# Weight splits that run further ahead into space that MoBA's values, outputs and softmax weights take later, in a two-layer trunk (mLSTM, MoBA)

## The chip, the cores and the metric

One core of a Trainium2 chip. The metric is the device time of one execution of the whole kernel in microseconds, as the median of several runs. The profile is of one further execution.

## What is computed

A residual trunk of two layers on 256 tokens of width 1024, all inputs float32. Each layer adds a token mixer and then a SwiGLU FFN of inner width 2816. Layer 0's mixer is a chunkwise mLSTM with 4 heads, layer 1's is MoBA block attention with 8 heads of 128; with 256 tokens there is one block, so it is causal attention with normed and partly rotated queries and keys.

```python
for layer in range(DEPTH):                       # DEPTH = 2
    u = rmsnorm(h, norm_mix[layer])
    y = mlstm_mixer(u, ...) if layer == 0 else moba_mixer(u, positions, ...)
    h = h + y
    h = h + swiglu(rmsnorm(h, norm_ffn[layer]), ffn_w_in[layer], ffn_w_out[layer])

def moba_mixer(u, positions, w_in, g_q, g_k, w_out):
    q, k, v = jnp.split(u @ w_in, 3, axis=-1)
    qh = rotary(rmsnorm(split_heads(q, h), g_q), positions, ROPE_DIMS, ROPE_THETA)
    kh = rotary(rmsnorm(split_heads(k, h), g_k), positions, ROPE_DIMS, ROPE_THETA)
    ...
    return merge_heads(softmax(causal(qh @ kh.T * scale)) @ vh) @ w_out
```

## The kernel before

**Products in three parts.** Every float32 product is made of float16 parts: a value is split into a high part h and a rest l, and the product is h·h + h·l + l·h, three matmuls into one PSUM bank. Matmuls are 128x128 against 512 columns; the activations are the stationary side (PEld), the weights move.

**Weight pieces.** All weight matrices are cut into 98 pieces of 1 MB (128 partitions x 2048 float32), in the order of use, the list `specs`. Layer 0 uses pieces 0 to 48, layer 1 pieces 49 to 97. Within a layer there are 12 pieces of the mixer's input projection, 4 of its output projection, 22 of the FFN's input and 11 of its output. In MoBA pieces 49 to 52 are queries and keys of the first four heads, 53 to 56 those of the others, 57 to 60 the values, 61 to 64 the output projection; 65 is the first of the second FFN.

**The class `Weights`** (from line 261) takes each piece through three stages. `load` and `quarter` bring it from HBM in four DMAs of 256 KB (a quarter), issued on SP's queue, into one of 5 buffers `raw`. `high` (line 286) makes half of the high part on ACT (`wh`, 128x1024), `low` (line 295) half of the rest on DVE (`wl`, 128x1024). So a piece costs two instructions on each of the two engines; pieces 0 and 1, at the start, are made in chunks by the hand-written list `START`. The split parts lie in a ring of `WBUFS` = 8 pieces (tags `wh` and `wl`). `take` hands pieces to a stage that is about to use them, and makes at once what isn't split yet; `free` gives them back once their last matmul is written. An output projection takes four pieces and frees them together at its end; the FFN's output stage frees its first seven one at a time and its last four, the tail, together.

**The order of the work** is set when the program is built, by a planner. `Pace` keeps a modelled time, `spend` advances it by the time of each group of matmuls, and after each such step it runs jobs that have come due. Chains (class `Chain`) are short sequences of DVE and ACT steps, such as a norm or a softmax; each step is due when its input is ready by the model. After each step `Weights.ahead` (line 312) may put in up to two quarters of loads, one `low` and one `high`. A split is put in only if its engine is free in the model and no chain step of that engine is due within `near` us (`pace.due`). `near` and `room` depend on the lead, the number of pieces split and not yet taken (line 321). Norm chains carry a margin of 1.25 us of their own, which `due` uses if it is larger than `near`. At the end, `in_queue_order` ties each engine's instructions to the order in which they were written. The instructions of SP's queue are in that order too: weight quarters, and the transposing DMAs.

**Flips.** `flip16` (line 510) transposes 16-bit tiles by DMA, on SP's queue. It follows the last step of a norm chain (`norm`, line 448), writing the next stage's activations `u` (`u_f<-n` in front of the FFNs, `u_b<-n` in front of MoBA), of MoBA's query and key chains (`bqT`, `bkT`), of softmax (`pT`) and of the FFN's hidden values (`h<-n`). The tile names of the profile are by the first program line that used a buffer, so that the norm's tile in front of layer 1's FFN is shown as `u_b<-x,r,grow`, and that in front of MoBA as `u_f<-x,r,grow`.

**The stages around the change.** `ffn(0, ...)`: the hidden stage (`gu`), then the output stage (`f0o`), then two norm chains, one for each token tile of 128. MoBA: `b` (query and key projections) with the chains of `qk_norm` (line 1054), the scores `s` and softmax chains of `softmax` (line 1113), `bv` (values, `v_done`, line 1108), `o` (attention times values, `attend_b`, line 1167), and `bo` (the output projection, `out_proj`, line 857). `out_proj` does token tile 0 first, adds the residual (`residual_half`), and starts its norm chain while PE works on token tile 1; then `ffn(1, ...)` begins with token tile 0 of the first hidden block. MoBA's tiles stand in the pool `pb`, among them the values `vb` (high and rest), the outputs `oh` and `ol`, and `pT` with 6 buffers.

```python
            lead = self.lows // 2 - self.taken
            near, room = (-9.0, 0.35) if lead < 2 else (0.7, 0.35) if lead < 3 else (1.6, 0.2) if lead < 5 else (3.0, 0.0)
            if self.lows < self.highs and pace.free["DVE"] <= pace.now + room and self.split[self.lows] < pace.now + 0.3 \
                    and not pace.due("DVE", near):
                self.low()
            if self.highs < 2 * (self.freed + WBUFS) and pace.free["ACT"] <= pace.now + room \
                    and self.loaded(self.highs // 2) and not pace.due("ACT", near):
                self.high()
```

Of the kernel before, what the change touches and what calls it, by code (L numbers as in the profile page):

```python
# [12 lines left out]
F16 = mybir.dt.float16  # L13
# [7 lines left out]
P = 128  # L21
D = 1024
KD = D // P
S = 256
NT = S // P
# [33 lines left out]
RAWBUFS, WBUFS = 5, 8  # L59
# [134 lines left out]
def in_queue_order(tc):  # L194

    last = {}
    for i in list(tc.nc.cur_bb.bb.instructions):
        if i.engine in last:
            tc.add_manual_dep(i, last[i.engine].name,
                              mybir.DependencyInfo(mybir.DependencyClass.NoSync, mybir.DependencyReason.DATA),  # L200
                              reason="queue order")
        last[i.engine] = i
# [3 lines left out]
def trunk(ctx: ExitStack, tc: tile.TileContext, a: dict, out: bass.AP):  # L206
    pace = Pace()
# [3 lines left out]
    wpool = ctx.enter_context(tc.tile_pool(name="wpool", bufs=1))  # L211
# [8 lines left out]
    def ybank(name):  # L220
        return py.tile([P, 512], F32, tag="y", name=name)

    def mm(dst, lhsT, rhs, start, stop):
        nc.tensor.matmul(dst, lhsT, rhs, start=start, stop=stop)  # L224
# [27 lines left out]
    specs = []  # L252
# [8 lines left out]
    class Weights:  # L261
        def __init__(self):
            self.raws, self.parts = [], []
            self.highs = self.lows = self.taken = self.freed = 0
            self.owed, self.landed, self.split = 0, {}, {}
            self.quarters = []

# [18 lines left out]
        def high(self):  # L286

            i, sl = self.highs // 2, self.half(self.highs)
            if i == len(self.parts):
                self.parts.append([wpool.tile([P, 2048], F16, tag=f"w{x}", bufs=WBUFS, name=f"w{x}{i}") for x in "hl"])  # L290
            nc.scalar.activation(self.parts[i][0][:, sl], self.raws[i][:, sl], AF.Copy, scale=WS)
            self.split[self.highs] = pace.end
            self.highs += 1
# [9 lines left out]
        def load_owed(self, whole=False):  # L303
            if self.owed and len(self.raws) < len(specs):
                self.load(whole)
                self.owed -= 1

        def loaded(self, i):

            return i < len(self.raws) and not any(q[0] <= i for q in self.quarters) and self.landed.get(i, 0.0) < pace.now + 0.3  # L310

        def ahead(self):

            for _ in range(2):
                if not self.quarters:
                    self.load_owed()
                if self.quarters and pace.free["DMA"] < pace.now + 0.5:
                    self.quarter()

            lead = self.lows // 2 - self.taken  # L320
            near, room = (-9.0, 0.35) if lead < 2 else (0.7, 0.35) if lead < 3 else (1.6, 0.2) if lead < 5 else (3.0, 0.0)
            if self.lows < self.highs and pace.free["DVE"] <= pace.now + room and self.split[self.lows] < pace.now + 0.3 \
                    and not pace.due("DVE", near):
                self.low()
            if self.highs < 2 * (self.freed + WBUFS) and pace.free["ACT"] <= pace.now + room \
                    and self.loaded(self.highs // 2) and not pace.due("ACT", near):
                self.high()

# [21 lines left out]
    ws = Weights()  # L350
# [45 lines left out]
    def new_u(name):  # L396

        both = act.tile([P, KD, 2, S], F16, tag="u16", bufs=1, name=f"u16_{name}")
        return both[:, :, 0, :], both[:, :, 1, :], both
# [110 lines left out]
    def flip16(dst, src):  # L510

        nc.sync.dma_start(dst, src, transpose=True)
        pace.work("DMA", 1.9, 1.3)
# [37 lines left out]
    for half in range(2):  # L551
        h = wpool.tile([P, 2048], F16, tag="wh", bufs=WBUFS, name=f"wh{half}")
# [3 lines left out]
    w = ws.take_k(2, 4)  # L556
# [173 lines left out]
    for g in range(2):  # L730
        w = ws.take_k(2, 4)
# [80 lines left out]
    for i in range(2):  # L812
        if i == 1:
            w = ws.take_k(2, 4)
# [34 lines left out]
    for i in range(2):  # L849
        w = ws.take_k(2, 4)  # L850
# [6 lines left out]
    def out_proj(name, y, ready, u_next, grow):  # L857

        w = []
        banks = [[xbank(f"{name}o{t}{n}") for n in range(2)] for t in range(NT)]  # L860

        def part(t, ks, ns=(0, 1)):
            for k in ks:
                if len(w) <= k:
                    w.extend(ws.take_k(1, 2))
                ready(t, k)
                acc_chunk(banks[t], *y(k), w[k], t, k == 0, k == KD - 1, ns)


        half = KD // 2  # L870
        part(0, range(half))
        part(1, range(half), (0,))
        ss = new_ss(0)
        sums = []
        for n in range(2):
            part(0, range(half, KD), (n,))
            sums.append(residual_half(0, n, banks[0][n], 1.0 / PS, ss))
        j0 = norm(name, 0, ss, grow, u_next, sums)
        ss = new_ss(1)
        sums = []  # L880
        for n in range(2):
            part(1, range(half if n == 0 else 0, KD), (n,))
            sums.append(residual_half(1, n, banks[1][n], 1.0 / PS, ss))
        j0()
        ws.free(4)
        return norm(name, 1, ss, grow, u_next, sums)
# [153 lines left out]
    def middle():  # L1040
        pace.later(1.0, rope_tables)

    u_next = new_u("b")
    j1 = ffn(0, u, j1, u_next, a["norm_mix"][1], middle)
    u = u_next
# [2 lines left out]
    pool_b = tc.tile_pool(name="pb", bufs=1)  # L1048
    pb = pool_b.__enter__()
    qkT = [pb.tile([P, 2, 8, S], F16, name=f"b{n}T") for n in "qk"]  # L1050
    vb = [pb.tile([P, NT, D], F16, name=f"vb{x}") for x in "hl"]
    tjobs = {}

    def qk_norm(g, i, t, b):
# [58 lines left out]
    def softmax(h):  # L1113

        for t in range(NT):
            for g in range(2):
                tjobs[g, h // 4, t].finish()
        b = ybank(f"s{h}")
        (qh, ql), (kh, kl) = [(x[:, h // 4, h % 4], x[:, h // 4, 4 + h % 4]) for x in qkT]
        for t in range(NT):  # L1120
            dst = b[:, t * P:t * P + (t + 1) * P]
            sl, ks = slice(t * P, (t + 1) * P), slice(0, (t + 1) * P)
            mm(dst, qh[:, sl], kh[:, ks], True, False)
            mm(dst, qh[:, sl], kl[:, ks], False, False)
            mm(dst, ql[:, sl], kh[:, ks], False, False)
            mm(b[:, 2 * t * P:(2 * t + 1) * P], identb, neg_ts, False, True)
        pace.spend(0.6)
        mx = small.tile([P, NT], F32, name="mx")
        p = pb.tile([P, 384], F32, tag="p", bufs=4, name="p")
        sm = small.tile([P, NT], F32, name="sm")  # L1130
        rs = small.tile([P, NT], F32, name="rsm")
        p16 = pb.tile([P, 2, 384], F16, tag="p16", bufs=3, name="p16")
        cols = (slice(0, 128), slice(128, 384))

        def biggest():
            for t in range(NT):
                nc.vector.tensor_reduce(mx[:, t:t + 1], b[:, cols[t]], axis=AX.X, op=ALU.max, negate=True)

        def exps():
            for t in range(NT):  # L1140
                nc.scalar.activation(p[:, cols[t]], b[:, cols[t]], AF.Exp, bias=mx[:, t:t + 1], accum_out=sm[:, t:t + 1])

        def factor():
            nc.vector.tensor_scalar(sm, sm, 1.0 / PSC, None, op0=ALU.mult)
            nc.vector.reciprocal(rs, sm)

        def high():
            for t in range(NT):
                nc.scalar.activation(p16[:, 0, cols[t]], p[:, cols[t]], AF.Copy, scale=rs[:, t:t + 1])

        def low():
            for t in range(NT):
                nc.vector.scalar_tensor_tensor(p16[:, 1, cols[t]], p[:, cols[t]], rs[:, t:t + 1], p16[:, 0, cols[t]],
                                               op0=ALU.mult, op1=ALU.subtract)
            pT = pb.tile([P, 2, 3, P], F16, tag="pT", bufs=6, name=f"pT{h}")
            flip16(pT.rearrange("p x c s -> p (x c) s"), p16.rearrange("p x n -> p (x n)"))
            pts[h] = [pT[:, x].rearrange("p c s -> p (c s)") for x in range(2)]

        last[0] = pace.now
        pace.end = pace.now + 0.15  # L1160
        fjobs[h] = Chain(pace, [("DVE", biggest), ("ACT", exps), ("DVE", factor), ("ACT", high), ("DVE", low)], True)

    fjobs = {}
    oh = pb.tile([P, KD, S], F16, name="oh")
    ol = pb.tile([P, KD, S], F16, name="ol")

    def attend_b(hp):
        b = ybank(f"o{hp}")
# [41 lines left out]
    for i in range(2):  # L1210
        w = ws.take_k(2, 4)
# [13 lines left out]
    u = new_u("f1")  # L1225
    j1 = out_proj("b", lambda k: (oh[:, k, :], ol[:, k, :]), ready_b, u, grow)
    pool_b.__exit__(None, None, None)
    ffn(1, u, j1, None, None, None)
    in_queue_order(tc)

# [20 lines left out]
```

## Time and profile before

| what | us |
|---|---|
| median of 3 runs | 551.24 |
| the runs | 548.90, 551.24, 552.22 |
| the profiled execution's own time | 550.87 |
| its span, from the first to the last instruction | 548.7 |
| PE busy in the span | 537.6 |
| DVE busy | 355.4 |
| ACT busy | 313.2 |

The profile's times are counted from the start of the span. PE is TensorE's matmuls, PEld its weight loads, DVE VectorE, ACT ScalarE, SPq the queue of the engine that issues the DMAs. A matmul's end is modelled and matmuls overlap, so 512 columns are shown as 0.38 us while one starts every 0.216 us. The waits name what ended an idle time: of several awaited things the one that came last by the profile. The chain of waits is followed back from the last instruction. "To landing" is the time from a DMA's issue to the arrival of its data. Nearly all instructions stand at one of two helper lines (L180 for ACT, DVE and POOL, L224 for matmuls), so the tile names tell them apart.

### The profile page before, as it was taken

How to read it: one execution, taken by the hardware profiler on the slowest of the kernel's cores; microseconds unless marked ns; L12 is line 12 of the kernel's file. 1: busy time of each engine (PE TensorE's matmuls, PEld its weight loads, DVE VectorE, ACT ScalarE, POOL GpSimd, SP SyncE). 2: the span in 40 equal slices, each digit the busy share in tenths (PEclk: the TensorE clock that was granted, in tenths of full speed). 3: DMA queues.
4: the chain of work that ended last, by engine and by line, in shares of the span. 5: the costliest groups of instructions: out<-in, count | busy, mean ns of one | idle time of the engine just before them, and what ended most of it. 6: DMA issues, size and time to landing. Idle time of an engine off the chain costs nothing.

```text
span 548.7 us, 7762 instructions
## 1 busy us (share of the span) xinstructions
PE 537.6 (98%) x2650; PEld 251.3 (46%) x2650; DVE 355.4 (65%) x540; ACT 313.2 (57%) x548; POOL 49.9 (9%) x105
## 2 busy tenths in 40 slices
PE   6999999999999999999999999998999999999997
PEld 2454654344444444444444455543444444444443
DVE  3889799478767665673358788998656647656201
ACT  5876794375466555563268996866455556456100
POOL 3600070020300000000013320000000000000000
PEclk8999999999999999999999999999999999999999
DMA  8999969959699787799328969798698888889002
GB/s 299 352 271 257 361 162 266 307 108 225 168 266 265 208 238 227 233 383 378 122 53 229 258 153 271 134 325 173 187 246 228 225 226 231 224 236 339 9 0 76
DMA packets 140679, 122.33 MB, mean 223 GB/s; under 512 B 66472, under 2 KB 111536, under 8 KB 140640
## 3 DMA queue, kind: packets, MB, share of 16 engines
q1 hardware_dynamic: 139904, 119.58, 77.6%
q0 software_dynamic: 736, 2.27, 1.5%
q8 instruction: 20, 0.33, 0.2%
q14 instruction: 19, 0.16, 0.1%
HBM read 106.08 MB, written 1.05 MB: 195 GB/s over the span
## 4 chain that ended last, share of the span: by engine, by line
PE 96%; DMA 1%; issue 1%; POOL 1%; DVE 0%; ACT 0%; SPq 0%; POOLq 0%; ACTq 0%
PE gu L224 42%; PE f1o L224 10%; PE f0o L224 10%; PE b L224 8%; PE ao L224 7%; PE av L224 4%; PE bo L224 4%; PE bv L224 4%; PE ak L224 2%; PE aq L224 2%; PE s L224 1%; PE num L224 1%; PE o L224 1%; DMA u_f<-n 1%; DMA x<-in_x 1%
## 5 line engine op out<-in xcount | busy, mean ns | idle before, releaser
L180 DVE SCALAR_TENSOR_TENSOR wl<-raw,wh 128x1024 f16<-128x1024 f32 (+1 forms) x200 | 236.9, 1203 | 43.0 <-ACT wh L180 41.5
L180 ACT ACTIVATE wh<-raw 128x1024 f16<-128x1024 f32 (+1 forms) x200 | 202.5, 1041 | 75.2 <-DMA raw<-in_ffn_w_in 32.9
L224 PE MATMUL gu<-wh,u_f 128*128 128x512 f16 x704 | 209.8, 379 | 3.1 <-DVE wl L180 1.9
L224 PEld LDWEIGHTS <-u_f 128*128 128x128 f16 x1056 | 103.2, 98 | 128.2 <-DMA u_f<-n 4.1
L224 PE MATMUL gu<-wl,u_f 128*128 128x512 f16 x352 | 133.4, 379 | 0.0
L224 PEld LDWEIGHTS <-h 128*128 128x128 f16 x528 | 51.7, 98 | 62.3
L180 DVE SCALAR_TENSOR_TENSOR fh<-gu,fsg 128x256 f32<-128x256 f32 x44 | 18.7, 425 | 55.9 <-ACT fsg L180 55.9
L224 PE MATMUL f1o<-wh,h 128*128 128x512 f16 x176 | 46.6, 379 | 0.0
L224 PE MATMUL f0o<-wh,h 128*128 128x512 f16 x176 | 46.6, 379 | 0.0
L224 PEld LDWEIGHTS <-u_a 128*128 128x128 f16 x336 | 29.2, 99 | 35.9 <-ACT u_a L180 3.1
L224 PEld LDWEIGHTS <-u_b 128*128 128x128 f16 x288 | 27.8, 98 | 32.0
L224 PE MATMUL b<-wh,u_b 128*128 128x512 f16 x128 | 38.9, 379 | 0.0
L180 ACT ACTIVATE fsg<-gu 128x256 f32<-128x256 f32 x44 | 16.7, 380 | 31.9 <-PE gu L224 31.7
L180 ACT ACTIVATE n<-fh 128x256 f16<-128x256 f32 x44 | 18.3, 416 | 18.3 <-DVE fh L180 18.2
L180 ACT ACTIVATE junk<-x 128x512 f32<-128x512 f32 x16 | 10.1, 630 | 31.0 <-DVE x L180 27.6
L224 PE MATMUL f0o<-wl,h 128*128 128x512 f16 x88 | 27.5, 379 | 0.0
L224 PE MATMUL f1o<-wl,h 128*128 128x512 f16 x88 | 27.5, 379 | 0.0
L224 PE MATMUL av<-wh,u_a 128*128 128x512 f16 x64 | 21.5, 398 | 2.9 <-ACT u_a L180 2.9
L224 PE MATMUL b<-wl,u_b 128*128 128x512 f16 x64 | 24.3, 379 | 0.0
L180 POOL TENSOR_TENSOR r<-s,mhalf 128x1 f32<-128x1 f32 x8 | 4.9, 609 | 211.4 <-DVE s L180 211.4
L180 DVE SCALAR_TENSOR_TENSOR x<-f1o,x 128x512 f32<-128x512 f32 x4 | 2.7, 689 | 31.5 <-PE f1o L224 31.5
L180 DVE TENSOR_TENSOR n<-fh,n 128x256 f16<-128x256 f32 x44 | 18.5, 421 | 2.4 <-ACT n L180 2.4
(178 smaller groups left out, 495.3 us busy)
## 6 DMA issues: line engine op xcount, KB each, us to landing
raw<-in_ffn_w_in SPq DMA_DIRECT2D x176, 256.0 KB, 4.4
raw<-in_ffn_w_out SPq DMA_DIRECT2D x88, 256.0 KB, 4.3
raw<-in_a_w_in SPq DMA_DIRECT2D x48, 256.0 KB, 5.4
raw<-in_b_w_in SPq DMA_DIRECT2D x48, 256.0 KB, 5.4
raw<-in_a_w_out SPq DMA_DIRECT2D x16, 256.0 KB, 5.3
raw<-in_b_w_out SPq DMA_DIRECT2D x16, 256.0 KB, 3.9
grow<-in_norm_ffn POOLq DMA_DIRECT2D x2, 512.0 KB, 5.6
out<-x SPq DMA_DIRECT2D x4, 256.0 KB, 2.0
```

The lines of the kernel that those rows point to most:

```text
L180: return fn(*args, **kw)
L224: nc.tensor.matmul(dst, lhsT, rhs, start=start, stop=stop)
```

## The change

`Weights` gets a table `outside` of pieces whose split parts don't lie in the ring. A tile `space` (three pieces' worth of float16, high and rest) is allocated before `ffn(0, ...)` and holds the parts of pieces 49, 50 and 51. The ring of 8 then counts only the others: `end_of_ring` gives the piece up to which highs may be made, walking from the first piece not freed over 8 ring pieces and any outside ones. Later MoBA puts its values into the first piece's space, its outputs into the second's, and `pT`, in 5 slots instead of 6 buffers, into the third's; `pb` no longer holds these. The thresholds of `near` and `room` move: 0.7 and 0.35 now hold for a lead of 2 to 4 (2 before), 1.6 and 0.2 for 5 and 6 (3 and 4 before), 3.0 and 0.0 from 7 on (from 5 on). They hold for the whole kernel. No instruction is added or taken away.

```diff
@@ class Weights
+            self.outside = {}
@@ high
             if i == len(self.parts):
-                self.parts.append([wpool.tile([P, 2048], F16, tag=f"w{x}", bufs=WBUFS, name=f"w{x}{i}") for x in "hl"])
+                self.parts.append(self.outside.get(i) or
+                                  [wpool.tile([P, 2048], F16, tag=f"w{x}", bufs=WBUFS, name=f"w{x}{i}") for x in "hl"])
@@
+        def end_of_ring(self):
+            end, ring = self.freed, WBUFS
+            while ring > 0 or end in self.outside:
+                ring -= end not in self.outside
+                end += 1
+            return end
@@ ahead
-            near, room = (-9.0, 0.35) if lead < 2 else (0.7, 0.35) if lead < 3 else (1.6, 0.2) if lead < 5 else (3.0, 0.0)
+            near, room = (-9.0, 0.35) if lead < 2 else (0.7, 0.35) if lead < 5 else (1.6, 0.2) if lead < 7 else (3.0, 0.0)
...
-            if self.highs < 2 * (self.freed + WBUFS) and pace.free["ACT"] <= pace.now + room \
+            if self.highs < 2 * self.end_of_ring() and pace.free["ACT"] <= pace.now + room \
@@ before ffn(0, ...)
+    pool_s = tc.tile_pool(name="ps", bufs=1)
+    space = pool_s.__enter__().tile([P, 3, 2, 2048], F16, name="space")
+    for i in range(3):
+        ws.outside[len(specs) // 2 + i] = [space[:, i, x] for x in range(2)]
@@ MoBA
-    vb = [pb.tile([P, NT, D], F16, name=f"vb{x}") for x in "hl"]
+    vb = [space[:, 0, x].rearrange("p (t n) -> p t n", t=NT) for x in range(2)]
@@ softmax, low
-            pT = pb.tile([P, 2, 3, P], F16, tag="pT", bufs=6, name=f"pT{h}")
+            n = h % 5 * 768
+            pT = space[:, 2].rearrange("p x n -> p (x n)")[:, n:n + 768].rearrange("p (x c s) -> p x c s", x=2, c=3)
@@
-    oh = pb.tile([P, KD, S], F16, name="oh")
-    ol = pb.tile([P, KD, S], F16, name="ol")
+    oh, ol = (space[:, 1, x].rearrange("p (k s) -> p k s", k=KD) for x in range(2))
@@ after MoBA's out_proj
     pool_b.__exit__(None, None, None)
+    pool_s.__exit__(None, None, None)
```

## Rows read from the trace of the kernel before

**Rows 1.** The page, part 1: busy time of PE and the other engines.
```profile
PE 537.6 (98%) x2650; PEld 251.3 (46%) x2650; DVE 355.4 (65%) x540; ACT 313.2 (57%) x548; POOL 49.9 (9%) x105
```

**Rows 2.** Waits of PE, whole span: waiter <- awaited: us in total, times, longest us.
```profile
PE av L224 <- ACT u_a L180: 2.9, 1, 2.9
PE gu L224 <- DVE wl L180: 1.9, 1, 1.9
PE gu L224 <- DMA u_f<-n: 1.3, 1, 1.3
...
```

**Rows 3.** The chain of waits, in order of time: start us, us, what.
```profile
105.35 3.81 DMA u_f<-n
...
280.31 33.67 PE b L224 x156
...
372.73 1.23 DVE wl L180
```

**Rows 4.** Timeline of PE at the two gaps: start us, us, what [idle before].
```profile
109.20 0.39 PE L224 MATMUL gu<-wh,u_f 128*128 128x512 f16 x1 [1.25 <-DMA u_f<-n]
...
371.71 0.38 PE L224 MATMUL bo<-wh,ol 128*128 128x512 f16 x1
373.94 0.39 PE L224 MATMUL gu<-wh,u_f 128*128 128x512 f16 x1 [1.85 <-DVE wl L180]
```

**Rows 5.** Timeline of PEld from 371.5 to 375.
```profile
373.93 0.98 PEld L224 LDWEIGHTS <-u_f 128*128 128x128 f16 x6 [2.34 <-DMA u_f<-n]
```

**Rows 6.** Flips to landing, by tile: `u_f` at 105.35, at 369.76, `u_b` at 275.14, all `bkT`.
```profile
DMA to landing us min/median/max: 3.8/3.8/3.8
...
DMA to landing us min/median/max: 4.1/4.1/4.1
...
DMA to landing us min/median/max: 3.2/3.2/3.2
...
DMA to landing us min/median/max: 3.3/3.5/5.7
```

**Rows 7.** Timeline of SP's queue, in front of 280 and of 372.
```profile
254.95 9.91 SPq L279 DMA_DIRECT2D raw<-in_b_w_in  x10
275.14 13.43 SPq L512 DMA_TRANSPOSE u_b<-n  x4
...
355.35 12.11 SPq L279 DMA_DIRECT2D raw<-in_ffn_w_in  x18
369.76 3.10 SPq L512 DMA_TRANSPOSE u_f<-n  x2
```

**Rows 8.** DMA issues from 264.2 to 265 and from 366.5 to 368: KB each, median us to landing.
```profile
raw<-in_b_w_in SPq DMA_DIRECT2D x2, 256.0 KB, 4.3
...
raw<-in_ffn_w_in SPq DMA_DIRECT2D x2, 256.0 KB, 5.9
```

**Rows 9.** DVE's `wl` splits by stretch: us, busy (count), PE's clock, DMA share, GB/s.
```profile
0.00:280.20 280.20, 127.97 (x110) 0.99 0.86 251
...
0.00:349.20 349.20, 152.00 (x130) 0.99 0.84 241
0.00:372.10 372.10, 165.15 (x141) 0.99 0.85 241
```

**Rows 10.** Engines by stretch: us, PE, PEld, DVE, ACT, POOL busy (count), clock, DMA share, GB/s.
```profile
263.20:280.20 17.00, 17.00 (x81) 7.69 (x79) 4.87 (x8) 4.38 (x9) 0.57 (x1) 1.00 0.36 94
280.20:324.00 43.80, 43.80 (x225) 21.01 (x224) 34.14 (x75) 37.69 (x113) 12.75 (x15) 1.00 0.74 193
```

**Rows 11.** The page, part 5: the two groups of splits (busy, mean ns of one | idle before).
```profile
L180 DVE SCALAR_TENSOR_TENSOR wl<-raw,wh 128x1024 f16<-128x1024 f32 (+1 forms) x200 | 236.9, 1203 | 43.0 <-ACT wh L180 41.5
L180 ACT ACTIVATE wh<-raw 128x1024 f16<-128x1024 f32 (+1 forms) x200 | 202.5, 1041 | 75.2 <-DMA raw<-in_ffn_w_in 32.9
```

**Rows 12.** Timeline of DVE: the residual add that starts each norm chain, layers 0 and 1.
```profile
100.22 0.69 DVE L180 SCALAR_TENSOR_TENSOR x<-ao,x 128x512 f32<-128x512 f32 x1 [1.90 <-PE ao L224]
...
364.64 0.68 DVE L180 SCALAR_TENSOR_TENSOR x<-bo,x 128x512 f32<-128x512 f32 x1
```

## The prediction

> **What bounds the kernel now.** I read the page's first part, then the waits of PE, the chain of waits, the timeline around each gap in it, and last the queue behind those gaps. The page says PE is busy for 537.6 of 548.7 us [rows 1]. A list of PE's waits has only four lines, three of which stand in [rows 2]: `av`'s (and the fourth, 1.2 us long, of the warm-up) belong to the start, whose hand-written order the change doesn't touch. The other two are the whole prize of the middle of the kernel, and both stand where a token mixer's output projection ends and an FFN begins. In layer 0 the first `gu` starts at 109.20, 1.25 us after the last `ao` matmul, which so ended at 107.95 [rows 2, 4]. In layer 1, the last `bo` ends at 371.71 + 0.38 = 372.09 and the first `gu` starts at 373.94, which is 1.85 us [rows 4]. After the start PE so waits 1.25 + 1.85 = 3.10 us in all, 0.56% of the span. MoBA itself (280.31 [rows 3] to 372.09) has no PE wait at all, although ACT and DVE are busiest there.
>
> **Which wait it is.** For layer 1 the chain names a `wl` split that ends at 372.73 + 1.23 = 373.96 [rows 3], which would suit the change well. The weight load of the same first matmul waited 2.34 us for the transposing DMA `u_f<-n` [rows 5]. Both end at one moment, so I counted pieces. By 349.2 DVE had started 130 `wl` instructions [rows 9]; 8 are the half-sized ones of pieces 0 and 1, the other 122 make 61 pieces, so all through piece 62 were split. By 372.1 there were 141 [rows 9], that is through 67 and half of 68. The matmul at 373.94 reads piece 65. So the `wl` is that of piece 68, and PE waits for the flip of the normed activations: issued at 369.76 [rows 7], landing 4.1 us later [rows 6], 373.9. In layer 0 it is the same: 105.35 [rows 3] + 3.8 [rows 6] = 109.15.
>
> So no late split stands on the path. A flip does, and its cost has two parts: when its chain (residual, squares, factor, scale, high, low) lets it be issued, and how much weight traffic is queued ahead. With a quiet queue the same flip took 3.2 us, at 275.14 [rows 6, 7]. In layer 1, SP had issued 18 weight quarters from 355.35 to 367.46 [rows 7], the last ones with 5.9 us to landing [rows 8]: the last lands near 373, the flip 0.9 us behind it. The Trainium skill ("DMA: Bandwidth & Descriptors", section "Queues, rings and completion order") says that each DMA engine consumes a ring's descriptors in ring order, so a transpose issued on SP's queue stands behind the loads issued before it. Layer 1's flip agrees (4.1 us against 3.2), and by that rule more loading ahead helps only where the loads end earlier, and hurts where they now end later; the second case is a rival below.
>
> **The change, part by part.**
>
> *Three pieces into `space`.* No instruction is added or removed: the split count stays at 200 on each engine, at 1203 ns on DVE and 1041 ns on ACT [rows 11]. What moves is pieces 53 to 55. Today the ring is full at about 263 (four tail pieces of f0o and 49 to 52: 110 `wl` by 280.2, so through piece 52 [rows 9]), and DVE and ACT work only 4.9 and 4.4 us of the 17 us from 263.2 to 280.2 [rows 10]. Six lows and six highs, 6 x 1.20 = 7.2 us of DVE and 6 x 1.04 = 6.2 us of ACT, go into those idle 12 us, and leave the stretch from 280.2 where ACT is at 37.7 of 43.8 us [rows 10]. On PE this is worth nothing directly, since PE waits for no split in MoBA. It is worth something at 372 alone: with three pieces in hand, the last splits before the ring limit (piece 68) and the loads that they set free come earlier, so the flip may meet a drained queue. Upper end: 4.1 - 3.2 = 0.9 us. Lower end: a queue still fuller; the longest landing of a flip of MoBA's keys is 5.7 [rows 6], 1.6 us worse. I take 0.9, since the only thing ahead of the flip is the burst, and a burst that ends 1 us sooner is enough (the last quarter at 373.0 would land at 372.0, the flip at 372.96 = 369.76 + 3.2); three pieces are worth far more than 1 us of DVE.
>
> *The chain in front of that flip.* The residual add of token tile 0 starts at 364.64, with no idle time in front of it, so behind a split [rows 12]; the last `bo` ends 7.45 us after it, where in layer 0 the same distance is 107.95 - 100.22 = 7.73 us [rows 4, 12]. So the splits delay the chain by 0.28 us; from the add to the flip both layers take 5.1 us. Without splits there the gain is at most 0.3; with more splits in the way it loses up to one split, 1.2 us. I take 0: a norm chain's steps keep their margin of 1.25 us in the planner, with or without the change.
>
> *Nearer splits.* A lead of 3 or 4 pieces now needs 0.7 us to the next chain step instead of 1.6, a lead of 5 or 6 needs 1.6 instead of 3.0. A split lasts 1.0 to 1.2 us, so a step may start up to 0.5 us late. Behind such steps stand PSUM banks and flips, with four banks per pool, and in the FFNs PE doesn't wait for them: rows 2 have no line for it. I take 0. At layer 0's gap (where the ring, 8 pieces behind the four that the output projection holds, bounds the splits too) the bounds are 3.8 - 3.2 = 0.6 gained and 5.7 - 3.8 = 1.9 lost; I take 0, since the threshold alone moves few splits there.
>
> *Values, outputs and softmax weights in `space`, `pT` with 5 slots instead of 6.* The old readers (b projections) are through before values are written, and slot 0 is wanted again by head 5, after head 0's product. I take 0 from both sides; one softmax flip late would cost what a flip costs, 3.2 us at most, once.
>
> *New traffic at 280.* Room for three more pieces also lets 12 more quarters be loaded before the f0o-to-MoBA boundary. Today the last quarters of that burst are issued by 254.95 + 9.91 = 264.86 [rows 7] and land 4.3 us later [rows 8], at 269.2. Twelve more at 0.67 to 0.99 us (12.11 / 18 and 9.91 / 10 [rows 7]) end at 277 to 281; the flip of `u_b`, issued at 275.14, would land 0.9 behind them, at 278 to 282, and PE needs it at 280.31 [rows 3]. Cost 0 to 1.6 us. I take 0, since the room opens before 263 and DMA is at 0.36 of its time from there to 280 [rows 10].
>
> **Sum.** -0.9 (flip at 372) + 0 + 0 + 0 + 0 = -0.9 us on the profiled execution's 550.87 us (span 548.7 and 2.17 around it): 549.97. The median of the three runs is 551.24, 0.37 above that execution, so on the median's scale 550.3.
>
> **Rivals.**
> 1. *Nothing moves.* The three pieces are eaten up in MoBA: once the lead is 2 or more, splits wait again for gaps, and by 349 the lead is back at its old two pieces (63 split, 61 used). The burst before 372 and the flip stay. For it: the lead is steered, not free. Against it: the looser threshold at a lead of 3 and 4. Time 551.2.
> 2. *Slower: the loads move the flip's wait to 280.* The extra quarters are still in SP's queue at 275, and `u_b` lands past 280.31, which decides from 280.31 - 275.14 = 5.2 us of landing on. For it: the ring order above, the count (277 to 281), one flip of 5.7 us. Against it: 280.31 - 275.14 - 3.2 = 2.0 us of slack today. Up to +1.6 us, with no gain at 372: 552.8.
> 3. *Both gaps shrink to what the chain itself leaves.* 0.9 + 0.3 at 372 and 0.6 at 108: -1.8, 549.4. For it: the looser rule also holds in layer 0. Against it: the first gap's splits are bound by the ring.
> 4. *Splits delay MoBA's chains so that scores wait.* Each of the 8 heads' chains late by 0.5 us and more, with flips behind them: 8 x 0.5 = 4 us and one flip of 3.2 make 558.4. Against it: fewer splits are left in MoBA, not more.
>
> **How the numbers follow.** Forecast 0.52, rival 1 0.25, rival 2 0.12, rival 3 0.08, rival 4 0.03. PE's waits in reach are 3.1 us in all, so faster by over 1% (5.5 us, about what a measurement of this kernel can tell from no change) can't come from the change: 0.02 for the spread of runs. Slower by over 1% needs rival 4 or the like: 0.04. Within 1%: 0.94. The runs spread by (552.22 - 548.90) / 2 = 1.7 us about their middle. Low end: rival 3 less that, 549.4 - 1.7 = 547.7, taken as 547.6. High end: no gain plus that, 552.9, and 0.5 into rival 2, 553.4.
>
> **What would show it.** Right: 116 `wl` by 280.2 instead of 110; the `gu` wait at 372 near 1 us and its flip's landing near 3.2; no new line in PE's waits; the gap at 108 near 1.25. Rival 1: landing still 4.1. Rival 2: a wait of `b` for `u_b<-n` at 280. The forecast is wrong if PE's wait list gets a new line over 1 us, or if the time moves by more than 3 us either way.

## The result, and the profile after

The changed kernel takes 552.37 us in the median of 16 executions (551.02 to 554.17), the kernel before, run beside it, 549.63 in 16 (547.43 to 552.22). The ratio is 1.0056, with a 95% interval of 1.0045 to 1.0067: slower by 0.56%, some 3 us. The profiled execution after took 554.17 us (span 552.5), the one before 550.87 (span 548.7); it is the slowest of its sixteen, so what is read from its trace below is more than the median execution lost.

PE's waits after the change (columns as in [rows 2]):

```profile
PE gu L224 <- DMA u_f<-n: 4.8, 2, 3.5
PE av L224 <- ACT u_a L180: 2.4, 1, 2.4
PE warm L224 <- DVE mhalf L180: 1.2, 1, 1.2
PE ut_a L507 <- DVE u_a L180: 0.5, 1, 0.5
```

They stand where they stood; the one of `ut_a` that has come in is short and belongs to the start. The `wl` that was named before is gone from the list, and both waits of `gu` are now put down to the flip `u_f<-n`: 4.8 us in two, the longer 3.5, so the first is 1.3 as before (1.25). The gap behind MoBA has grown from 1.85 to 3.46 us:

```profile
374.78 0.61 PE L224 MATMUL gu<-wh,u_f 128*128 128x512 f16 x1 [3.46 <-DMA u_f<-n]
```

The chain of waits after (start us, us, what) shows a second loss:

```profile
104.61 3.85 DMA u_f<-n
108.51 114.13 PE gu L224 x528
...
369.08 5.65 DMA u_f<-n
374.78 117.02 PE gu L224 x528
491.80 56.99 PE f1o L224 x264
```

The flip that landed 4.1 us after its issue [rows 6] now takes 5.65. And the 528 `gu` matmuls behind it take 117.02 us, where the first FFN's take 114.13. In the kernel before, the same stretch was:

```profile
373.96 114.11 PE gu L224 x528
```

That makes the spans' difference of 552.5 - 548.7 = 3.8 us: +1.6 for the gap, +2.9 for `gu`, and -0.7 at the start (in the chain `aq` begins at 25.28 before and at 24.55 after, behind the hand-written order that the change doesn't touch; over the other profiles it begins between 23.97 and 26.27, so this part is scatter). Why `gu` is slower can be read in the stretches around the gap, first before, then after (us, busy time of PE, PEld, DVE, ACT, POOL with counts, granted clock, DMA share, GB/s):

```profile
372.10:373.90 1.80, 0.00 (x0) 0.00 (x0) 1.77 (x3) 0.99 (x3) 0.00 (x0) 1.00 0.83 177
373.90:380.00 6.10, 6.06 (x29) 2.76 (x30) 4.33 (x8) 5.79 (x8) 0.56 (x1) 1.00 0.99 229
```

```profile
371.30:374.70 3.40, 0.02 (x1) 0.00 (x0) 1.82 (x4) 2.56 (x4) 0.56 (x1) 0.87 1.24 203
374.70:380.00 5.30, 5.22 (x13) 1.92 (x14) 3.02 (x4) 3.55 (x5) 0.00 (x0) 0.50 0.51 90
380.00:385.00 5.00, 5.00 (x23) 2.13 (x22) 1.53 (x3) 1.94 (x3) 0.00 (x0) 0.93 0.14 26
385.00:390.00 5.00, 5.00 (x25) 2.27 (x24) 3.98 (x6) 3.33 (x6) 0.00 (x0) 1.00 0.27 65
```

Before, the granted clock stays at 1.00 through the 1.85 us without matmuls. After, it falls within the 3.46 us and stands at 0.50, the 1.2 GHz level, in the FFN's first 5.3 us: 13 matmuls there, where 29 went through in 6.1 us. That is also why PE is shown as busy while it loses time.

The kernel before has such a fall too, though not at the two gaps: at its start, behind the 2.9 us wait of `av` [rows 2], the clock stands at 0.50 until 16 us, and matmuls start 0.43 us apart instead of 0.22. The stretch around it (mean clock 0.68):

```profile
10.00:20.00 10.00, 9.41 (x33) 4.16 (x34) 8.96 (x24) 9.32 (x27) 9.20 (x16) 0.68 1.05 353
```

The queue in front of the flip, in the timeline of SP's queue after (compare [rows 7]):

```profile
245.00 19.89 SPq L281 DMA_DIRECT2D raw<-in_b_w_in  x29
274.42 12.46 SPq L522 DMA_TRANSPOSE u_b<-n  x4
...
350.92 17.25 SPq L281 DMA_DIRECT2D raw<-in_ffn_w_in  x22
369.08 10.33 SPq L522 DMA_TRANSPOSE u_f<-n  x4
```

Before, 18 weight quarters were issued, the last by 367.46, and four more only after token tile 0's two flips; the flip stood 2.3 us behind the last quarter. Now there are 22, the last by 368.17, 0.9 us ahead of the flip. In the order of SP's queue, 71.75 pieces had been loaded ahead of that flip before, and 74 are now: the most that the ring and the 5 `raw` buffers let in at that place.

How far the splits ran can be counted as in [rows 9] (DVE's `wl` from the start to a time):

```profile
0.00:279.60 279.60, 126.94 (x110) 0.99 0.90 263
...
0.00:348.60 348.60, 146.17 (x126) 0.99 0.87 246
...
0.00:371.00 371.00, 157.92 (x136) 0.99 0.87 247
```

The six lows of pieces 49 to 51 bear another tile name now, and have to be added:

```profile
L180 DVE SCALAR_TENSOR_TENSOR space<-raw,space 128x1024 f16<-128x1024 f32 x6 | 6.9, 1218 | 0.0
```

So 116 lows were done when MoBA began, against 110 [rows 9], 132 when its output projection began (130), and 142 at the gap (141; 140 when the flip was issued). The change does what it says: three pieces more at 280. But MoBA's stages eat two thirds of that by 349, and when the flip is issued a lead of two lows, one piece, is left.

### The profile page after: what moved, and what is told of

Its sections match the earlier page's. It is cut to its first block, busy times and chain, and to the rows that moved or that the text cites. A ratio compares the mean times of both kernels' runs of the same rounds, so it can differ in the third digit from the quotient of the medians.

```text
span 552.5 us, 7757 instructions
## 1 busy us (share of the span) xinstructions
PE 539.7 (98%) x2650; PEld 252.1 (46%) x2650; DVE 356.1 (64%) x540; ACT 308.5 (56%) x548; POOL 47.9 (9%) x105
## 4 chain that ended last, share of the span: by engine, by line
PE 93%; DMA 2%; DVE 2%; issue 1%; POOL 1%; ACT 1%; DVEq 0%; SPq 0%; ACTq 0%; POOLq 0%
PE gu L224 42%; PE f1o L224 10%; PE f0o L224 10%; PE b L224 8%; PE ao L224 7%; PE av L224 4%; PE bv L224 4%; PE ak L224 2%; PE aq L224 2%; DMA u_f<-n 2%; DVE wl L180 1%; PE bo L224 1%; PE s L224 1%; PE num L224 1%; PE o L224 1%
## 5 line engine op out<-in xcount | busy, mean ns | idle before, releaser
L180 DVE SCALAR_TENSOR_TENSOR wl<-raw,wh 128x1024 f16<-128x1024 f32 (+1 forms) x194 | 226.7, 1202 | 34.0 <-ACT wh L180 33.8
L180 ACT ACTIVATE wh<-raw 128x1024 f16<-128x1024 f32 (+1 forms) x194 | 194.1, 1036 | 44.9 <-DMA raw<-in_ffn_w_in 18.2
L224 PE MATMUL b<-wh,u_b 128*128 128x512 f16 x80 | 24.8, 379 | 0.0
L224 PE MATMUL bv<-wh,u_b 128*128 128x512 f16 x64 | 20.0, 379 | 0.0
```

The costliest lines, as they stand in the source:

```text
L180: return fn(*args, **kw)
```

## Experiments

Two theories were set against each other. Q: the loss sits in SP's queue at the gap behind MoBA; more quarters are issued close ahead of the flip, it lands later, and PE's clock falls. N: splits that stand nearer to chain steps delay the chains.

**The thresholds alone**, in the kernel before.

```diff
-            near, room = (-9.0, 0.35) if lead < 2 else (0.7, 0.35) if lead < 3 else (1.6, 0.2) if lead < 5 else (3.0, 0.0)
+            near, room = (-9.0, 0.35) if lead < 2 else (0.7, 0.35) if lead < 5 else (1.6, 0.2) if lead < 7 else (3.0, 0.0)
```

> The kernel before with the new thresholds of near and room alone; no space outside the ring. Theory Q (the loss sits at the layer-1 flip: more weight quarters stand ahead of it in SP's queue, PE waits longer, and its clock falls): in program order 70.75 pieces are loaded ahead of that flip, against 71.75 in the kernel before and 74 in the changed one, so its landing is at most 4.1 us, PE's wait at the gap 1.9 us or less, granted clock 1.0 after it, time 548 to 550, not slower than before. Theory N (splits nearer to chain steps delay the chains): slower by 1 to 3 us, with the flip issued later against the end of bo.

Measured: 549.71 us, ratio 1.0008 (0.9991 to 1.0025), so the thresholds by themselves cost nothing that can be told. SP's queue and PE at the gap:

```profile
354.29 12.15 SPq L279 DMA_DIRECT2D raw<-in_ffn_w_in  x18
369.36 2.61 SPq L512 DMA_TRANSPOSE u_f<-n  x2
```

```profile
372.91 0.39 PE L224 MATMUL gu<-wh,u_f 128*128 128x512 f16 x1 [1.22 <-DMA u_f<-n]
```

The last quarter is issued by 366.44, 2.9 us ahead of the flip, which lands after 3.5 us. N is out for the thresholds. One small wait of its kind did appear, 0.7 us of the scores for a key flip:

```profile
PE s L224 <- DMA bkT<-n: 0.7, 1, 0.7
```

**The space alone**: the changed kernel with the old thresholds.

```diff
-            near, room = (-9.0, 0.35) if lead < 2 else (0.7, 0.35) if lead < 5 else (1.6, 0.2) if lead < 7 else (3.0, 0.0)
+            near, room = (-9.0, 0.35) if lead < 2 else (0.7, 0.35) if lead < 3 else (1.6, 0.2) if lead < 5 else (3.0, 0.0)
```

> The changed kernel with the old thresholds: only the three pieces outside the ring and MoBA's tiles in their space. 73 pieces are loaded ahead of the layer-1 flip (before 71.75, changed 74). Theory Q: landing between 4 and 5.6 us, PE's wait 1.9 to 3 us, time 549.5 to 551.5, between the two kernels. Theory N: as fast as before, 549 to 550, with the wait as before.

Measured: 550.31 us, ratio 1.0018 (1.0004 to 1.0032), between the two kernels and nearer to the old one. In its profile 73 pieces are ahead of the flip, but the last quarter leaves by 366.59, 2.8 us before it; landing 3.5, and PE waits 1.74.

```profile
352.05 14.54 SPq L281 DMA_DIRECT2D raw<-in_ffn_w_in  x20
369.38 2.62 SPq L522 DMA_TRANSPOSE u_f<-n  x2
```

```profile
372.92 0.39 PE L224 MATMUL gu<-wh,u_f 128*128 128x512 f16 x1 [1.74 <-DMA u_f<-n]
```

Landing and wait are both below what Q expected, and that shows that the count of pieces is not what decides but how near to the flip the last ones are issued. The remaining 0.2% isn't explained by this profile, which took 549.41 itself.

The two halves of the change work together. When the flip was issued, 139 lows were done in near_only, 140 in the kernel before, 141 in space_only and 142 in the changed kernel, with 70.75, 71.75, 73 and 74 pieces ahead of it: neither half alone lets piece 73 in.

**The suspected quarters held back**: the changed kernel, in which piece 73 is loaded only after token tile 0's flips.

```diff
-            self.owed, self.landed, self.split = 0, {}, {}
+            self.owed, self.landed, self.split, self.hold = 0, {}, {}, 73
...
-            if self.owed and len(self.raws) < len(specs):
+            if self.owed and len(self.raws) < len(specs) and len(self.raws) != self.hold:
...
         j0()
+        if name == "b":
+            ws.hold = None
         ws.free(4)
```

> The changed kernel, but the four quarters of piece 73 are issued only after token tile 0's flips at the end of MoBA's output projection; nothing else changes until then. Theory Q: the flip's landing falls from 5.65 by up to 4 x 0.75 = 3 us, to between 3.2 and 4.2, PE's wait from 3.5 to between 1 and 2, clock 1.0 after it, time 547.5 to 549.5. Theory N: the chain, not the queue, is late; no more than 0.5 us better than the changed kernel.

Measured: 549.03 us, ratio 0.9992 (0.9975 to 1.0009). The loss is gone, by four DMAs that were moved past two others.

```profile
351.23 14.24 SPq L281 DMA_DIRECT2D raw<-in_ffn_w_in  x18
369.39 2.62 SPq L522 DMA_TRANSPOSE u_f<-n  x2
372.06 2.13 SPq L281 DMA_DIRECT2D raw<-in_ffn_w_in  x4
```

```profile
369.39 3.20 DMA u_f<-n
372.64 114.13 PE gu L224 x528
```

The last quarter goes out 3.9 us ahead of the flip, the flip lands after 3.2 us as with a quiet queue, PE waits 1.01 us and `gu` takes its 114.13. As all else of the change is still in this kernel, the space and the thresholds cost nothing that can be told beside these quarters. A small cost isn't excluded: PE's wait is 0.84 us shorter here than in the kernel before, and the median is only 0.4 us lower than that of the kernel before run beside it (549.42).

**The gap filled**: the changed kernel with spare matmuls behind the last `bo`, so that PE is busy while it waits.

```diff
         j0()
+        if name == "b":
+            idle = ybank("idle")
+            for _ in range(16):
+                mm(idle, y(KD - 1)[0][:, 0:P], w[-1][0][:, 0:512], True, True)
```

> The changed kernel with 16 spare matmuls (128x512, result unused) written behind the last bo, 16 x 0.216 = 3.45 us of PE work in the gap; the schedule of everything else is the planner's as before up to there. If the longer half of the loss is the clock that falls after the idle gap (gu 117.0 us instead of 114.1): granted clock stays 1.0 after the gap, gu's stretch is 114.1, time 1.5 to 3 us below the changed kernel, 549.5 to 551. If the clock falls for another reason: no change, or up to 0.5 us slower.

Measured: 551.33 us, ratio 1.0040 (1.0026 to 1.0054). The gap is as long, but the clock stays up:

```profile
371.30:375.00 3.70, 3.70 (x18) 1.56 (x16) 1.77 (x4) 2.51 (x4) 0.56 (x1) 1.00 1.23 259
375.00:380.00 5.00, 5.00 (x24) 2.27 (x24) 3.07 (x4) 3.60 (x5) 0.00 (x0) 1.00 0.51 99
```

```profile
375.12 114.08 PE gu L224 x528
```

The direction is as expected and `gu` is back at 114.08, but the gain of 1.0 us in the medians is less than the 1.5 to 3 that were expected, and the intervals of this and of the changed kernel overlap. So the pair was measured again on one chip:

> The changed kernel itself, unaltered, on the same chip as busy_same: a ratio of 1.0045 to 1.0067 as measured.

> The changed kernel with the 16 spare matmuls in the gap, beside the changed kernel: the difference of the two is the clock's part of the loss in the median execution. By the profile of the changed kernel (gu 117.0 instead of 114.1) up to 2.9 us; by the first pair of ratios (1.0056 and 1.0040) 0.9 us. A value near 0 would take the clock out of the cause.

Measured: the changed kernel 553.40 us, ratio 1.0050 (1.0028 to 1.0072); with spare matmuls 551.73, ratio 1.0031 (1.0011 to 1.0050). The clock's part is so about 1.0 us by the ratios (0.0019 x 549.6) and 1.7 by the medians; in both pairs the sign is the same, but the intervals overlap. `gu` in the two profiles, first of the changed kernel, then with spare matmuls:

```profile
374.75 115.82 PE gu L224 x528
```

```profile
376.74 114.05 PE gu L224 x528
```

The size differs from execution to execution: in the repeated profile of the changed kernel `gu` took 115.82 us, in the first 117.02.

**The loss made without the change**: the kernel before, with the quarters of pieces 71 and 72 written right ahead of the flip.

```diff
-            self.owed, self.landed, self.split = 0, {}, {}
+            self.owed, self.landed, self.split, self.hold = 0, {}, {}, 71
...
-            if self.owed and len(self.raws) < len(specs):
+            if self.owed and len(self.raws) < len(specs) and len(self.raws) != self.hold:
...
                 nc.vector.scalar_tensor_tensor(l, v, c, h, op0=ALU.mult, op1=ALU.subtract)
+                if name == "b" and t == 0 and j == 0:
+                    ws.hold = None
+                    ws.load_owed(True)
+                    ws.load_owed(True)
                 flip16(...)
```

> The kernel before, with none of the change, but with the quarters of pieces 71 and 72 written right ahead of token tile 0's flip at the end of MoBA's output projection (73 pieces ahead of it instead of 71.75). Theory Q: the last quarter is issued about 1 us ahead of the flip instead of 2.3, the flip lands 5 to 6 us after its issue, PE waits 2.8 to 3.7 us, the granted clock falls to 1.2 GHz after the gap in some executions; time 1.5 to 3 us over the kernel before, so most of the change's loss without the change. If something else of the change made the loss (the space, the thresholds): within 0.5 us of the kernel before.

Measured: 555.80 us, ratio 1.0105 (1.0076 to 1.0133), twice the loss of the change, and more than was expected. The last quarter was issued only by 370.20, so the flip itself left late: 0.5 us before the end of `bo`, where in the kernel before it left 2.3 us before it. And it landed after 6.0 us.

```profile
354.43 15.77 SPq L279 DMA_DIRECT2D raw<-in_ffn_w_in  x23
370.63 11.19 SPq L516 DMA_TRANSPOSE u_f<-n  x4
```

```profile
370.63 6.00 DMA u_f<-n
376.68 116.35 PE gu L224 x528
```

PE waits 5.56 us, 3.7 more than in the kernel before: 1.9 of that is the longer landing and 1.8 the late issue, so only half of it repeats what the change did. The clock falls here too, and `gu` loses 116.35 - 114.13 = 2.2 us.

```profile
376.60:380.00 3.40, 3.32 (x8) 1.19 (x9) 2.41 (x3) 2.99 (x4) 0.00 (x0) 0.50 0.63 71
```

With 26 spare matmuls in that gap, and nothing else changed:

> push72 with 26 spare matmuls (5.6 us of PE work, result unused) in its gap of 5.56 us. If the idle gap makes the clock fall and that costs what the rows of push72 show (gu's stretch 116.35 instead of 114.13): clock 1.0 after the gap, gu 114.1, and about 2.2 us off push72's loss of 1.05%, so a ratio near 1.0065 to the kernel before, from the wait alone. If the clock is no cause: 1.0105 as before.

Measured: 553.60 us, ratio 1.0066 (1.0044 to 1.0089), as expected; 0.0039 x 549.6 = 2.1 us are the clock's. `gu` is back at 114.13:

```profile
354.43 15.27 SPq L279 DMA_DIRECT2D raw<-in_ffn_w_in  x23
370.14 11.64 SPq L516 DMA_TRANSPOSE u_f<-n  x4
```

```profile
370.14 7.55 DMA u_f<-n
377.74 114.13 PE gu L224 x528
```

One thing in this profile was not expected: the flip, again 0.4 us behind the last quarter, took 7.55 us to land instead of 6.0, and PE was idle for 1.18 us behind the spare matmuls. The last two quarters ahead of it took 7.5 us to landing too, where they took 5.9 in push72. Why is open.

**Both gaps cleared**, with the change and without it: pieces held back behind token tile 0's flips at the end of both output projections (24 and 73 in the changed kernel, 24 and 71 in the kernel before).

```diff
-            self.owed, self.landed, self.split = 0, {}, {}
+            self.owed, self.landed, self.split, self.hold = 0, {}, {}, dict(a=24, b=73)
...
-            if self.owed and len(self.raws) < len(specs):
+            if self.owed and len(self.raws) < len(specs) and len(self.raws) not in self.hold.values():
...
         j0()
+        ws.hold.pop(name)
         ws.free(4)
```

> The changed kernel with piece 73 held back as in hold73, and in the same way piece 24 behind token tile 0's flips at the end of layer 0's output projection. Theory Q: there too the flip lands after 3.2 instead of 3.8 us, PE's wait falls from 1.25 to about 0.7; with 1.0 at the second gap the time is 0.6 below hold73, 548.4, and about 1 us below the kernel before. If the first gap is set by the chain alone: as hold73, 549.0.

> The kernel before with pieces 24 and 71 held back behind token tile 0's flips at the two gaps; no space, old thresholds. Theory Q: landing 3.2 at both, waits 0.7 and 1.0 to 1.3, time 1.0 to 1.4 below the kernel before; equal to hold_both within 0.5 us, as the extra space is worth nothing by itself. If running three pieces ahead has a worth of its own once the queue is out of the way, hold_both is the faster of the two by more than 0.5 us.

Measured: 548.93 us, ratio 0.9986 (0.9968 to 1.0003) with the change; 548.26 us, ratio 0.9964 (0.9942 to 0.9985) without it. PE's waits with the old kernel:

```profile
PE gu L224 <- DMA u_f<-n: 1.6, 2, 0.9
```

```profile
355.22 9.26 SPq L279 DMA_DIRECT2D raw<-in_ffn_w_in  x15
369.56 2.61 SPq L512 DMA_TRANSPOSE u_f<-n  x2
```

Both flips land after 3.2 us, in either kernel; the two waits together are 1.6 us (old_hold) and 1.7 (hold_both) instead of 3.1. The kernel before with two pieces held back is the fastest of all. The extra space adds nothing to it; if anything, hold_both is the slower one, but the intervals overlap. Its median came out at 548.93, not at the 548.4 expected, and lies 0.7 us above that of old_hold, where no more than 0.5 either way was expected. With the 0.2% of space_only and the small shortfall of hold73 this leans the same way each time; whether the space or the thresholds cost some half a microsecond of their own is not shown.

The runs without spare matmuls in one table, ordered by how long before the flip behind MoBA the last quarter was issued (from the timeline of SP's queue of each kernel):

| kernel | pieces ahead of the flip | last quarter before the flip, us | landing, us | PE's wait, us | ratio |
|---|---|---|---|---|---|
| old_hold | 71 | 5.1 | 3.2 | 0.93 | 0.9964 |
| hold_both | 73 | 3.9 | 3.2 | 1.02 | 0.9986 |
| hold73 | 73 | 3.9 | 3.2 | 1.01 | 0.9992 |
| near_only | 70.75 | 2.9 | 3.5 | 1.22 | 1.0008 |
| space_only | 73 | 2.8 | 3.5 | 1.74 | 1.0018 |
| before | 71.75 | 2.3 | 4.1 | 1.85 | 1 |
| after_same (the changed kernel again) | 74 | 1.1 | 5.5 | 3.31 | 1.0050 |
| changed | 74 | 0.9 | 5.65 | 3.46 | 1.0056 |
| push72 | 73 | 0.4 | 6.0 | 5.56 | 1.0105 |

The landing follows the third column, in old and new kernels alike; the flip of push_busy, 7.55 us at a distance of 0.4, is the one that doesn't. PE's wait is the landing less the time by which the flip was issued ahead of the end of `bo`: 1.8 us in space_only, 2.3 in the kernel before, 0.5 in push72.

## Why the prediction was wrong

- *What bounds the kernel* held: after the change PE's waits are in the same two places, MoBA has none of its own, and the flip, not the `wl`, was the one to look at. The attribution to `wl` in [rows 2] was a coincidence of two ends; in no later profile is it named at this gap.
- *Three pieces into `space`* is the step that failed: "I take 0.9, since the only thing ahead of the flip is the burst, and a burst that ends 1 us sooner is enough". I took the burst as a fixed amount of loading that a faster DVE would bring to an earlier end. It isn't fixed. Each piece whose second low is made frees a `raw` buffer and so lets four more quarters be issued, and in this stretch a quarter takes 5.9 us to landing [rows 8]. Being further on therefore put more quarters ahead of the flip, 22 instead of 18, and the last of them nearer to it, 0.9 us instead of 2.3. The landing went from 4.1 to 5.65 us, not to 3.2. The lower end that was named for this term, a landing of 5.7 us, was nearly what came, but in the sum and the chances it had no weight.
- *No term for the clock.* I priced a longer wait at its own length. The granted clock falls in the longer gap and costs a further 1.0 to 1.7 us in the median execution and 2.9 in the profiled one. Together with the gap's 1.6 us that makes 2.6 to 3.3, against a measured 2.7 by the medians and 3.1 by the ratio. At the two gaps the trace before shows no such fall, but its start shows the one told above, behind a wait of 2.9 us [rows 2], and that could have been priced. The Trainium skill says ("TensorE: Matmul & The Clock Gate", section "What's actually happening") that a clock gate sets the array's clock by how busy PE has been recently; the rows after agree, 0.50 behind 3.46 us without matmuls. It would have been the rule to weigh against this change.
- *Nearer splits* at nothing: held, 1.0008 (0.9991 to 1.0025).
- *Values, outputs, softmax weights in `space`* at nothing: held within the noise, as hold73 has them all and is at 0.9992 (0.9975 to 1.0009).
- *New traffic at 280*, and rival 2 that was built on it: it was the right mechanism at the wrong place. 29 quarters were issued there by 264.89, and the flip of `u_b` at 274.42 came in time; PE has no wait for it. The same ring order decided 100 us later.
- Rival 1 described the lead rightly (116 lows at 280, but only 132 against 130 at 349), and its conclusion, that the burst before 372 stays, was too mild: two lows more at the flip (142 against 140) were enough to let the last piece in ahead of it.
- The layer-0 gap stayed at 1.3 us, as forecast; old_hold and hold_both show that 0.6 us could be had there by the queue alone.

The measured 552.37 lies within the stated range, and within 1% of before, but the forecast was a gain of 0.9 us and the change loses some 3. That the range held is luck: it was laid about a median of three executions, 551.24, where sixteen give 549.63, and its upper end stands for no gain and the scatter of those three, not for a loss of this kind. Of the signs that were named, the 116 lows, the first gap and the list of waits without a new long line came; the landing near 3.2 and the wait near 1 us did not.

## What to carry to other kernels

Where prefetches and a transfer on the critical path share a queue, running further ahead is not free even when every buffer has room: the question is what is issued in the last few microseconds before that transfer. Hold the prefetch back behind it for that moment; here four DMAs moved past two others were worth the whole loss of the change, and the old kernel with that alone, done at both gaps, beat both. And price a longer wait of PE with the clock behind it, not by its own length.

## What the runs showed that I had not expected

- The flip's landing follows one line in all profiles but one. In the burst a quarter takes about 5.9 us to landing [rows 8], so a last quarter issued d before the flip lands 5.9 - d after the flip's issue, and the flip some 0.5 us behind it, but never under the 3.2 us of a quiet queue: at 0.4, 0.9, 2.3 and 2.9 us this gives 6.0, 5.5, 4.1 and 3.5, measured 6.0, 5.65, 4.1 and 3.5; from 3.2 us of distance on there is, by this estimate, nothing more to gain (3.9 and 5.1 us gave 3.2). I had put the flip 0.9 us behind. At layer 0's gap distance and landing add up to nearly the same, 6.4 to 6.8 us in the ten kernels that hold nothing back there (2.95 and 3.8 in the kernel before). The exception is push_busy: 0.4 and 7.55.
- At the gap behind MoBA the granted clock fell after idle gaps of 3.3 to 5.6 us, and at neither gap after 1.85 us or less. The length of one gap doesn't tell all: at the kernels' start, where the matmuls stand thinner, the clock was at 0.50 behind a wait of `av` of 2.9 us in the kernel before and of 1.2 us in space_only. The loss behind it wasn't the same each time: `gu` took 115.82, 116.35 and 117.02 us instead of 114.13, at gaps of 3.31, 5.56 and 3.46 us, so the longest gap wasn't the dearest. Spare matmuls in the gap kept the clock at 1.00 in all three kernels that had them.
